# Adding a convolution's taps by accumulating transfers on GpSimd's queue instead of on VectorE

## The chip, the core and the metric

The kernel runs as one launch on one core of a Trainium2 chip (trn2). The metric is the device time of the launch in microseconds (us). The engines are named as in the profile: PE is TensorE (its weight loads are PEld), DVE is VectorE, ACT is ScalarE, POOL is GpSimd, and SP is SyncE, which here only issues transfers. Each engine works through its own instructions in the order in which they were written; across engines and transfers only semaphores order the work.

## What is computed

A decoder trunk of two layers over 256 tokens of width 2048: a gated-linear-attention layer, then a forgetting-attention layer, both with a cross attention into 256 memory tokens, and a channel mixer at the end of each layer. The change touches the channel mixers alone, which are in essence:

```
def causal_dwconv(u, w, b):          # u: (1, 256, 11264)
    up = pad(u, two zero rows ahead)
    return w[0] * up[:, 0:s] + w[1] * up[:, 1:s+1] + w[2] * up[:, 2:s+2] + b

def conv_ffn(h, w_up, conv_w, conv_b, w_down):
    u = causal_dwconv(h @ w_up, conv_w, conv_b)
    a, val = split(u, 2)             # 5632 columns each
    return (silu(a) * val) @ w_down
```

Every column of `h @ w_up` is thus filtered along the tokens with three taps of its own and a bias. All matrix products keep close to full fp32 accuracy: an operand is split into a rounded high part and a low part, and a product is hi*hi + lo*hi + hi*lo on PE.

## The kernel before

**Weights.** The weights stream from HBM in units of 128x1024 words (512 KB). For each unit (`split_unit`, L210 to L235) SP issues the load into one of four `raw` buffers, ACT makes the high part (`whi<-raw`, L233), DVE subtracts it to get the low part (`wlo<-raw,whi`, L234), and PE multiplies with both; `whi` and `wlo` have four buffers each. A cast can thus start when its load has landed and PE has finished with the `whi` of four units ago, and a load can be issued when DVE has finished with the `raw` of four units ago. The casts are issued with a high priority, and the other work of ACT and DVE is tied behind one of them by `tc.issue_after(casts[-1].ins)` or `tc.issue_after(lows[-1].ins)`, so the order of ACT and DVE is, step by step, a cast and then the small work of that step.

**The channel mixer** (`ffn`, L1394). An up step (`up_pair`, L1493) multiplies the 256 tokens with 16 units of `w_up`, in matmuls of 512 columns (L412); one or two pairs of units in it are done with seven block products in place of eight (line L382 casts their weights, L437 to L440 form their sums on DVE). It yields two *turns*, each with two gate and two value chunks of 128 columns. The columns have to lie on the partitions before the convolution and the next product, so each turn is transposed: DVE transposes 32x32 blocks (L1464), POOL's queue sends the tile to HBM and brings it back rearranged (`far_away`, one 512 KB transfer `far<-yu` at L650 and four of 128 KB at L655, `fvt<-far` in the first layer, `yzu<-far` in the second).

**The taps.** When a turn is back, ACT scales it with each tap's weight into three tiles, `tap0` to `tap2` (twelve instructions of 128x256 at L1414: two chunks, gate and value, three taps); `tap1` and `tap2` hold the data shifted by one and two tokens, with zeros ahead. DVE adds `tap1` and then `tap2` to `tap0` in place (`add_tap`, L1421, 128x1024 each). ACT applies silu to the gate half (L1427), DVE multiplies it with the value half (`cv<-tap`, L1434), and the product is split in high and low part (L528 on ACT, L529 on DVE), which become operands of the down product. One set of tap tiles serves all turns.

**What sets the order.** `tick` (L1479) runs once a unit of weights: it gives a credit (1.45, or 1.7 and 2.4 in places) and takes steps from the front of one queue, `waiting`, while credit is left. A tap costs 0.5, an addition 1.0, silu 0.5, the gating 1.0 and 0.7. A turn may be fetched back three ticks after it was sent, and its steps start 8 (or 7) ticks after that, if the steps of the turns before have been taken. There are 44 chunks of columns, so 22 turns in each layer.

## Time and profile before

| | |
|---|---|
| median of 3 runs | 2211.19 us (2211.04 to 2212.21) |
| span of the profiled execution, first to last instruction | 2210.2 us, 1.0 us less than the median |
| PE busy | 2199.2 us |
| DVE busy | 1793.1 us |
| ACT busy | 1421.8 us |
| POOL busy | 136.5 us |
| moved by transfers | 515.41 MB |
| granted TensorE clock | 0.999 of full speed |

The profiled execution is one execution of the program, and the runs are timed apart from it. In the rows of the profile, `L412` is a line of the kernel, `out<-in` are its tiles without their buffer numbers, and `x264` is a count. In a row of a group of instructions, the busy time in us and the mean duration of one in ns follow the first bar, and the idle time of the engine just before them, with what ended it, follows the second. In a timeline a row begins with its start and its duration in us, and a bracket holds the idle time before it and what ended it. A matmul's end is modelled in the profile, so PE's real pace is read from the number of matmuls in a stretch.

### The profile page before, as it was taken

The page shows a single profiled execution, that of the slowest core. Times are in us where ns is not written, and L with a number is a line of the kernel's source. Part 1 is how long each engine was busy: PE and PEld are TensorE (multiplying, and loading weights), DVE is VectorE, ACT ScalarE, POOL GpSimd, SP SyncE. Part 2 cuts the span into 40 slices and gives each one's busy share as a digit, 9 for nine tenths or more (in the row PEclk, how much of TensorE's full clock was granted, in tenths as well). Part 3 has the DMA queues.
Part 4 walks back from the last instruction along what each step waited for, and adds up shares of the span by engine and source line. Part 5 has one row for each costly group of instructions (what it writes and reads, how often), then busy time and mean ns, then how long its engine had stood idle before and what let it go on. Part 6 is the DMA issues. An engine that isn't in the chain of part 4 may idle for free.

```text
span 2210.2 us, 30065 instructions
## 1 busy us (share of the span) xinstructions
PE 2199.2 (100%) x10315; PEld 1851.8 (84%) x10315; DVE 1793.1 (81%) x2655; ACT 1421.8 (64%) x2260; POOL 136.5 (6%) x257
## 2 busy tenths in 40 slices
PE   9999999999999999999999999999999999999998
PEld 7888888888888888888888998888888888888886
DVE  7768977688897889888978669668888888988896
ACT  6655664566787567656865555555788656765874
POOL 0000000001100000001110000000100000100100
PEclk9999999999999999999999999999999999999999
DMA  9867567777677567667678767677777657776774
GB/s 343 259 224 224 190 194 236 252 232 253 227 243 265 187 219 233 231 234 247 222 244 265 231 201 243 225 239 241 228 241 248 234 187 237 243 247 224 227 259 153
DMA packets 166289, 515.41 MB, mean 233 GB/s; under 512 B 20780, under 2 KB 42552, under 8 KB 166136
## 3 DMA queue, kind: packets, MB, share of 16 engines
q1 hardware_dynamic: 149064, 460.99, 63.1%
q0 software_dynamic: 16496, 51.71, 7.5%
q8 instruction: 81, 1.33, 0.2%
q10 hardware_dynamic: 576, 0.79, 0.1%
q14 instruction: 72, 0.59, 0.1%
HBM read 469.62 MB, written 43.79 MB: 232 GB/s over the span
## 4 chain that ended last, share of the span: by engine, by line
PE 99%; DVE 1%; ACT 0%; issue 0%; DVEq 0%; ACTq 0%
PE acc L412 29%; PE acc L338 26%; PE ps_s L412 15%; PE ps_o L412 8%; PE ps_t L412 7%; PE acc L309 3%; PE acc L264 3%; PE ps_s L338 2%; PE acc L368 2%; PE acc L262 1%; PE ps_s L1035 0%; PE ps_o L701 0%; PE ps_s L701 0%; PE ps_s L1308 0%; PE ps_s L1081 0%; PE ps_o L1263 0%
## 5 line engine op out<-in xcount | busy, mean ns | idle before, releaser
L234 DVE TENSOR_TENSOR wlo<-raw,whi 128x1024 fp32r<-128x1024 f32 (+2 forms) x705 | 841.2, 1203 | 241.3 <-ACT whi L233 220.7
L233 ACT ACTIVATE whi<-raw 128x1024 fp32r<-128x1024 f32 (+2 forms) x705 | 729.8, 1046 | 405.4 <-PE acc L338 131.9
L338 PE MATMUL acc<-whi,B 128*128 128x512 f32 (+3 forms) x1248 | 291.7, 370 | 0.0
L382 ACT ACTIVATE whi<-raw 128x1024 fp32r<-128x1024 f32 (+1 forms) x144 | 137.0, 954 | 197.4 <-PE acc L412 75.4
L338 PEld LDWEIGHTS acc<-whi,B 128*128 128x128 f32 x1248 | 226.8, 188 | 28.1
L412 PE MATMUL acc<-whi,mix 128*128 128x512 f32 x756 | 192.9, 389 | 0.0
L412 PE MATMUL acc<-whi,B 128*128 128x512 f32 x738 | 189.8, 389 | 0.0
L383 DVE TENSOR_TENSOR wlo<-raw,whi 128x1024 fp32r<-128x1024 f32 (+1 forms) x144 | 156.2, 1089 | 40.3 <-ACT whi L382 37.2
L412 PEld LDWEIGHTS acc<-whi,mix 128*128 128x128 f32 x756 | 141.9, 188 | 29.5
L412 PEld LDWEIGHTS acc<-whi,B 128*128 128x128 f32 x738 | 138.5, 188 | 28.7
L338 PE MATMUL acc<-wlo,B 128*128 128x512 f32 (+3 forms) x624 | 158.5, 369 | 0.0
L338 PEld LDWEIGHTS acc<-wlo,B 128*128 128x128 f32 x624 | 114.5, 188 | 14.6
L1414 ACT ACTIVATE tap<-fvt,cw 128x256 f32<-128x256 f32 x264 | 123.5, 531 | 2.6 <-DMA fvt<-far 2.5
L1414 ACT ACTIVATE tap<-yzu,cw 128x256 f32<-128x256 f32 x264 | 123.5, 531 | 2.0 <-DMA yzu<-far 2.0
L1421 DVE TENSOR_TENSOR tap<-tap,tap 128x1024 f32<-128x1024 f32 x88 | 107.2, 1219 | 1.4 <-ACT tap L1414 1.0
L412 PE MATMUL ps_s<-whi,mix 128*128 128x512 f32 x386 | 106.2, 389 | 0.0
L412 PE MATMUL acc<-wlo,mix 128*128 128x512 f32 x378 | 105.6, 389 | 0.0
L412 PE MATMUL acc<-wlo,B 128*128 128x512 f32 x369 | 105.1, 389 | 0.0
L412 PE MATMUL ps_s<-whi,B 128*128 128x512 f32 x342 | 93.1, 389 | 0.0
L412 PEld LDWEIGHTS ps_s<-whi,mix 128*128 128x128 f32 x386 | 72.5, 188 | 15.0
L412 PEld LDWEIGHTS acc<-wlo,mix 128*128 128x128 f32 x378 | 70.9, 188 | 14.7
L412 PEld LDWEIGHTS acc<-wlo,B 128*128 128x128 f32 x369 | 69.3, 188 | 14.4
(502 smaller groups left out, 3866.5 us busy)
## 6 DMA issues: line engine op xcount, KB each, us to landing
raw<-wp SPq DMA_DIRECT2D x741, 512.0 KB, 4.6
fvt<-far POOLq DMA_DIRECT2D x100, 128.0 KB, 5.5
raw<-wp SPq DMA_DIRECT2D x32, 384.0 KB, 3.5
far<-yu POOLq DMA_DIRECT2D x22, 512.0 KB, 5.3
far<-yzu POOLq DMA_DIRECT2D x22, 512.0 KB, 5.3
yzu<-far POOLq DMA_DIRECT2D x88, 128.0 KB, 5.5
raw<-wp SPq DMA_DIRECT2D x24, 388.0 KB, 4.4
x<-xtok SPq DMA_DIRECT2D x8, 512.0 KB, 7.2
```

Of the source, the lines that this page charges most:

```text
L233: casts.append(S.activation(hi[:, s], raw[:, s], AF.Copy))
L234: lows.append(V.tensor_tensor(lo[:, s], raw[:, s], hi[:, s].bitcast(F32), ALU.subtract))
L262: mm = TE.matmul(acc[p][c][:, :T], w[:, s], both[:, 0, :], start=False, stop=end and j == 3)
L264: mm = TE.matmul(acc[p][c], w[:, s], both, start=u == j == 0, stop=end and j == 3)
L309: mm = TE.matmul(acc[b][:, :n], src[kcs[j] - base][:, part, b * P : (b + 1) * P], w, start=u == 0 and low == part == j == 0, stop=u == end ...
L338: mm = TE.matmul(acc[b][:, :n], src[kc - base][:, part, b * P : (b + 1) * P], ready[low][:, j * room : j * room + n], start=i == low == pa ...
L368: mm = TE.matmul(acc[b][:, :n], src[kc - base][:, part, b * P : (b + 1) * P], w, start=i == low == part == j == 0, stop=i == end and low = ...
L382: casts.append(S.activation(hi[:, :n], src, AF.Copy))
L383: lows.append(V.tensor_tensor(lo[:, :n], src, hi[:, :n].bitcast(F32), ALU.subtract))
L412: r = TE.matmul(bank[name], x, w, start=name not in begun, stop=last)
L1414: S.activation(by_run(taps[i][:, s, c, i:]), zs[slot][:, :, 2 * c + s], AF.Copy if i else AF.Identity, bias=0.0 if i else w[3], scale=w[2 ...
L1421: V.tensor_tensor(taps[0], taps[0], taps[n][:, :, :, :T], ALU.add)
```

## The change

The two additions of a turn no longer run on DVE. They are two transfers from SBUF to SBUF on POOL's queue which add what they carry to the destination (`accum_op=ALU.add`): first `tap1` onto the sum, then `tap2` onto the sum. Each carries a whole tile, 128x1032 words, 528 KB: all tap tiles get the width 258 for each of their four rows of 256 tokens so that source and destination are flat and of one size, and POOL zeroes the parts that no tap writes. The last two turns of each layer (`j` of 40 and 42) still add on DVE.

The sum has two tiles now, `taps[0]` and `taps[3]`, that serve the turns by turns (`summed(slot)`); `tap1` and `tap2` still have one tile each. The twelve taps are written in another order: `tap0` and `tap1` first, then `tap1` is added, then `tap2` is written and added. Silu and gating go into a second queue of steps, `rear_steps`, and become due four ticks (`ADDED`) after the second addition was issued; `tick` takes a due step of that queue before one of `waiting`. An addition by transfer costs no credit. Finally the program is built with 4096 bytes of SBUF in each partition for the descriptors of POOL's transfers, where it had no such setting before.

On ACT the change moves the taps and silu. This is the piece of the first layer where two turns follow each other; in the kernel before, L233 is the cast, L1414 a tap, L1427 silu, L528 the split of a product:

```order
L528 ACTIVATE A_95<-cv 128x256
L528 ACTIVATE A_96<-cv 128x256
L1414 ACTIVATE tap_4593<-fvt,cw 128x4x2x32 x3
L233 ACTIVATE whi<-raw 128x1024
L1414 ACTIVATE tap_4593<-fvt,cw 128x4x2x32
L233 ACTIVATE whi<-raw 128x1024 x3
L1414 ACTIVATE tap_4594<-fvt,cw 128x4x2x32
L233 ACTIVATE whi<-raw 128x1024
L1414 ACTIVATE tap_4594<-fvt,cw 128x4x2x32 x2
L1427 ACTIVATE tap_4593<-tap_4593 128x2x256
```

Here `tap_4593` is `tap0` and the sum of every turn, and `tap_4594` is `tap1`: the first turn's `tap0` comes last, three casts stand between it and the next turn's first `tap1`, and silu follows. After the change, behind the first turn's last `tap1`, stands this on ACT (L235 is the cast, L1421 a tap, L530 the split; `tap_4594` is `tap1`, `tap_4595` is `tap2`, `tap_4593` the second turn's sum):

```order
L530 ACTIVATE A_95<-cv 128x256
L530 ACTIVATE A_96<-cv 128x256
L235 ACTIVATE whi<-raw 128x1024
L1421 ACTIVATE tap_4595<-fvt,cw 128x4x2x32 x3
L235 ACTIVATE whi<-raw 128x1024
L1421 ACTIVATE tap_4595<-fvt,cw 128x4x2x32
L235 ACTIVATE whi<-raw 128x1024 x2
L1421 ACTIVATE tap_4593<-fvt,cw 128x4x2x32 x4
L235 ACTIVATE whi<-raw 128x1024
L1421 ACTIVATE tap_4594<-fvt,cw 128x4x2x32 x4
L235 ACTIVATE whi<-raw 128x1024 x2
L1421 ACTIVATE tap_4595<-fvt,cw 128x4x2x32 x2
```

The second turn's `tap1` now overwrites what the first turn's first transfer reads, with five casts between, and its `tap2` overwrites what the first turn's second transfer reads.

On POOL, before, the turns alone went out and back:

```order
L650 DMA far<-yu 128x1024
L655 DMA fvt<-far 32x4x256 x4
L650 DMA far<-yu 128x1024
L655 DMA fvt<-far 32x4x256 x4
L650 DMA far<-yu 128x1024
```

After the change, two turns out and back are followed by their four additions, each in the same queue (`tap_4596` is the first turn's sum):

```order
L652 DMA far<-yu 128x1024 x2
L657 DMA fvt<-far 32x4x256 x8
L1429 DMA tap_4596<-tap_4594 128x1032
L1429 DMA tap_4596<-tap_4595 128x1032
L1429 DMA tap_4593<-tap_4594 128x1032
L1429 DMA tap_4593<-tap_4595 128x1032
L652 DMA far<-yu 128x1024
L657 DMA fvt<-far 32x4x256 x4
```

The queue gains 80 transfers in all, and DVE loses 80 of its 88 additions. PE's matmuls, ACT's instructions and SP's transfers keep their numbers.

The whole diff:

```diff
--- before.py
+++ after.py
@@ -36,6 +36,8 @@
 SEVEN_DOWN = {4: 0, 10: 1, 20: 0, 34: 1}
 SEVEN_MORE = 11
 MORE_IN = (5, 6, 8)
+ADDED = 4
+SCRATCH = 4096
 
 
 LEVELS = (64, 16, 4)
@@ -1400,38 +1402,50 @@
             rooms = {i: held("dsum", i) for i in range(2)}
             cw = fp.tile([P, 4 * 88], F32, name="cw")
             nc.sync.dma_start(cw, cnv[l])
-            taps = [fp.tile([P, 2, 2, T + i], F32, name=f"tap{i}") for i in range(3)]
-            for i in (1, 2):
-                nc.gpsimd.memset(taps[i][:, :, :, :i], 0.0)
+            taps = [fp.tile([P, 2, 2, T + 2], F32, name=f"tap{i}") for i in range(4)]
+            for i in range(4):
+                nc.gpsimd.memset(taps[i] if i in (0, 3) else taps[i][:, :, :, : T + 2 : T + 1] if i == 1 else
+                                 taps[i][:, :, :, :i], 0.0)
             count = [0, 0, 0]
             sums = {}
 
+            def summed(slot):
+                return taps[3 * slot]
+
             def tap_of(j, s, c, i, slot):
 
+                t = taps[i] if i else summed(slot)
                 col = (c * 44 + j + s) * 4
                 w = [cw[:, col + n : col + n + 1] for n in range(4)]
                 with tc.issue_after(casts[-1].ins):
-                    S.activation(by_run(taps[i][:, s, c, i:]), zs[slot][:, :, 2 * c + s], AF.Copy if i else AF.Identity,
+                    S.activation(by_run(t[:, s, c, i : T + i]), zs[slot][:, :, 2 * c + s], AF.Copy if i else AF.Identity,
                                  bias=0.0 if i else w[3], scale=w[2 - i])
                 unread[slot] -= 1
 
-            def add_tap(n):
-
+            def add_tap(n, slot, far):
+
+                t = summed(slot)
+                if far:
+                    sent.append(nc.gpsimd.dma_start(flat_tap(t), flat_tap(taps[n]), accum_op=ALU.add))
+                    return
                 with tc.issue_after(lows[-1].ins):
-                    V.tensor_tensor(taps[0], taps[0], taps[n][:, :, :, :T], ALU.add)
-
-            def silu():
-
-                t = taps[0][:, :, 0, :]
+                    V.tensor_tensor(t[:, :, :, :T], t[:, :, :, :T], taps[n][:, :, :, :T], ALU.add)
+
+            def flat_tap(t):
+                return t.rearrange("p s c t -> p (s c t)")
+
+            def silu(slot):
+
+                t = summed(slot)[:, :, 0, :T]
                 with tc.issue_after(casts[-1].ins):
                     S.activation(t, t, AF.Silu)
 
-            def gated(j, s):
+            def gated(j, s, slot):
 
                 if s == 0:
                     product[0] = fp.tile([P, 2, T], F32, name="cv", tag="cv")
                     with tc.issue_after(lows[-1].ins):
-                        V.tensor_tensor(product[0], taps[0][:, :, 0, :], taps[0][:, :, 1, :], ALU.mult)
+                        V.tensor_tensor(product[0], summed(slot)[:, :, 0, :T], summed(slot)[:, :, 1, :T], ALU.mult)
                 r = product[0]
                 with tc.issue_after(lows[-1].ins):
                     split(m, (j + s) % RING, r[:, s, :])
@@ -1465,15 +1479,25 @@
                     if b:
                         away = far_away(dram, flat(y), T, nc.gpsimd)
                         back = lambda: away(flat(z))
-                        steps = [(0.5, lambda s=s, c=c, i=i: tap_of(j, s, c, i, slot)) for n in ((1, 2), (0,))
-                                 for s in range(2) for c in range(2) for i in n]
-                        steps += [(1.0, lambda: add_tap(1)), (1.0, lambda: add_tap(2)), (0.5, silu),
-                                  (1.0, lambda: gated(j, 0)), (0.7, lambda: gated(j, 1))]
+                        far = j < HID // P - 4
+
+                        def taps_of(*n):
+                            return [(0.5, lambda s=s, c=c, i=i: tap_of(j, s, c, i, slot))
+                                    for s in range(2) for c in range(2) for i in n]
+
+                        def ended():
+                            add_tap(2, slot, far)
+                            rear_steps.extend((clock[0] + (ADDED if far else 0), *step) for step in (
+                                (0.5, lambda: silu(slot)), (1.0, lambda: gated(j, 0, slot)),
+                                (0.7, lambda: gated(j, 1, slot))))
+
+                        cost = 0.0 if far else 1.0
+                        steps = [*taps_of(0, 1), (cost, lambda: add_tap(1, slot, far)), *taps_of(2), (cost, ended)]
                         returns.append((clock[0] + 3, slot, back, [(clock[0] + wait, *step) for step in steps]))
 
                 return evac
 
-            waiting, clock, credit = [], [0], [0.0]
+            waiting, rear_steps, clock, credit = [], [], [0], [0.0]
             returns, unread, turned_last = [], [0, 0], [None]
 
             def tick(share):
@@ -1485,8 +1509,11 @@
                     back()
                     unread[slot] = 12
                     waiting.extend(steps)
-                while waiting and waiting[0][0] <= clock[0] and credit[0] > 0:
-                    _, cost, step = waiting.pop(0)
+                while credit[0] > 0:
+                    ready = [q for q in (rear_steps, waiting) if q and q[0][0] <= clock[0]]
+                    if not ready:
+                        break
+                    _, cost, step = ready[0].pop(0)
                     credit[0] -= cost
                     step()
 
@@ -1573,7 +1600,7 @@
                 tick(2.4)
             for _ in wide:
                 tick(2.4)
-            assert not waiting and not returns
+            assert not waiting and not returns and not rear_steps
             if l:
                 for u in range(3, 8):
                     f2(u)
@@ -1787,7 +1814,7 @@
         "par": par,
         "msk": _constants(),
     }
-    nc = bacc.Bacc("TRN2", target_bir_lowering=False, num_devices=1)
+    nc = bacc.Bacc("TRN2", target_bir_lowering=False, num_devices=1, dynamic_dma_scratch_size=SCRATCH)
     aps = [nc.dram_tensor(n, v.shape, mybir.dt.from_np(v.dtype), kind="ExternalInput").ap()
            for n, v in arrays.items()]
     aps.append(nc.dram_tensor("out", (2, P, D), F32, kind="ExternalOutput").ap())
```

## The prediction

> **What bounds the kernel now.** I read the page's busy times first, then PE's waits, then stretches of the two channel mixers, then ACT's timeline in a stretch full of taps.
>
> ```profile
> span 2210.2 us, 30065 instructions
> PE 2199.2 (100%) x10315; PEld 1851.8 (84%) x10315; DVE 1793.1 (81%) x2655; ACT 1421.8 (64%) x2260; POOL 136.5 (6%) x257
> PE ps_o L183 <- DVE B L180: 1.5, 1, 1.5
> PE acc L412 <- ACT whi L382: 0.7, 1, 0.7
> 1922.58 32.64 PE acc L412 x144
> 517.70:1118.60 600.90, 600.19 (x2648) 496.42 (x2647) 515.44 (x607) 423.09 (x642) 56.17 (x103) 1.00 0.70 232
> 1559.00:2140.00 581.00, 581.00 (x2565) 481.07 (x2564) 499.40 (x590) 408.09 (x614) 54.73 (x100) 1.00 0.71 235
> ```
>
> The second row gives each engine's busy time: PE is never free, DVE is free for a fifth. Rows three and four are all of PE's waits: 1.5 us at the start and 0.7 us once in a channel mixer. As a matmul's end is modelled, I check by counting. The chain's row has 144 matmuls in 32.64 us, 0.2267 us each. The last two rows are the stretches from the first to the last tap of the two mixers (length; then busy time and count of PE, PEld, DVE, ACT, POOL; clock; busy share of the transfer engines; GB/s). The first holds 2648 matmuls, and 2648 x 0.2267 = 600.2 of its 600.9 us; the second holds 2565, or 581.4 of 581.0. So PE runs at its own pace, at full clock, and DVE's additions are on no path that sets the end. All that this change can win is that 0.7 us.
>
> What it can lose depends on how far the casts run ahead of PE. ACT's timeline, at a point where two turns' taps are written:
>
> ```profile
> 595.52 1.06 ACT L382 ACTIVATE whi<-raw 128x1024 fp32r<-128x1024 f32 x1 [2.09 <-PE ps_t L412]
> ...
> 600.11 1.06 ACT L382 ACTIVATE whi<-raw 128x1024 fp32r<-128x1024 f32 x1 [2.49 <-DVE raw L438]
> ...
> 602.04 1.06 ACT L382 ACTIVATE whi<-raw 128x1024 fp32r<-128x1024 f32 x1 [0.25 <-DVE raw L440]
> 603.01 1.05 ACT L233 ACTIVATE whi<-raw 128x1024 fp32r<-128x1024 f32 x1
> ...
> 605.00 1.30 ACT L1414 ACTIVATE tap<-fvt,cw 128x256 f32<-128x256 f32 x3
> 606.20 1.05 ACT L233 ACTIVATE whi<-raw 128x1024 fp32r<-128x1024 f32 x1
> 607.15 1.30 ACT L1414 ACTIVATE tap<-fvt,cw 128x256 f32<-128x256 f32 x3
> ...
> 625.16 0.71 ACT L528 ACTIVATE mix<-cv 128x256 fp32r<-128x256 f32 x2
> 625.78 0.59 ACT L1414 ACTIVATE tap<-fvt,cw 128x256 f32<-128x256 f32 x1
> ...
> 630.20 1.07 ACT L233 ACTIVATE whi<-raw 128x1024 fp32r<-128x1024 f32 x1 [0.46 <-PE acc L412]
> 590.23 1.22 DVE L1421 TENSOR_TENSOR tap<-tap,tap 128x1024 f32<-128x1024 f32 x1
> 595.03 1.22 DVE L1421 TENSOR_TENSOR tap<-tap,tap 128x1024 f32<-128x1024 f32 x1
> ```
>
> At 595.52 and 630.20 the cast waited for PE to free a buffer, so there it was as far ahead as four buffers allow. In between it was not. The cast at 595.52 opens when PE has left the `whi` of four units ago; ahead of it stand two whole units and a half-wide one of the seven-product pair (12, 12 and 3 matmuls) and the 4 low matmuls of the unit being left: 31 x 0.2267 = 7.0 us, so PE needs it at 602.5. The two casts after it serve 6 matmuls each, as it does, so the cast of 603.01 is needed 18 x 0.2267 = 4.1 us later, at 606.6, and that of 606.20 one unit (2.7 us) later, at 609.3. They end at 604.1 and 607.3: a lead of 2.0 to 2.5 us. It is short because the cast at 600.11 waited 2.49 us for DVE's weight sums, and ahead of these DVE had just done two of the additions that now go (2.4 us, the last two rows).
>
> **The change part by part.**
>
> *What goes from DVE.* The far turns are those with `j` below 40: 20 a layer, 40 in all, two additions each.
>
> ```profile
> L1421 DVE TENSOR_TENSOR tap<-tap,tap 128x1024 f32<-128x1024 f32 x88 | 107.2, 1219 | 1.4 <-ACT tap L1414 1.0
> far<-yu POOLq DMA_DIRECT2D x22, 512.0 KB, 5.3
> far<-x SPq DMA_DIRECT2D x8, 512.0 KB, 3.4
> fvt<-far POOLq DMA_DIRECT2D x100, 128.0 KB, 5.5
> q0 software_dynamic: 16496, 51.71, 7.5%
> 594.03 2.18 POOL L655 DMA_DIRECT2D fvt<-far  x4 [5.28 <-DMA far<-yu]
> 632.42 0.56 POOL L650 DMA_DIRECT2D far<-yu  x1 [25.28 <-DVE yu L1464]
> ```
>
> 80 x 1.219 = 97.5 us leave DVE. All of it was beside PE's work, so it is worth nothing by itself; it only lengthens the lead where DVE was late, by up to the 2.4 us above. I take a lead of 3 us in such a stretch.
>
> *What comes: 80 accumulating transfers of 528 KB.* No row shows one. From below I bound its landing by the quickest 512 KB rows, SP's store at 3.4 us. From above: q0 is POOL's queue, and 7.5% of 16 engines' span of 2210.2 us for 51.71 MB makes 2652 engine-us, 27.1 for 0.528 MB, or 1.7 us of all 16 engines. If adding costs as much as three more passes, it lands after 5.3 + 3 x 1.7 = 10.4 us. I take one more pass, since the destination has to be read too: 5.3 + 1.7 = 7.0 us, with the row of the same queue and nearly the same size as its base.
>
> The Trainium skill ("Collectives: The Full Stack", section "The bandwidth ceiling: the fold count and why AG ≠ RS ≠ AR") says that an addition inside a transfer costs no cycles but needs two source reads, which halves the rate; no run here shows it. Its page "DMA: Bandwidth & Descriptors" (section on the anatomy of one SWDGE transfer) fits 2.0 us + bytes/436e3, an estimate of 3.2 us for 528 KB, or 4.4 with a second read; then ACT would not wait at all. The trace has 5.3 us for the plain transfer of 512 KB beside the weight stream, so the page's floor is too low here.
>
> *Where ACT waits for them.* On ACT, after the first turn's last `tap1`, stand (order above) a pair of splits, five casts, four `tap2` and four first taps of the second turn before its first `tap1`. By the timeline's starts a cast takes 0.95 us, a tap 0.40 and the pair 0.62: 0.62 + 5 x 0.95 + 8 x 0.40 = 8.6 us. The first transfer has landed by then (7.0). Up to the second turn's first `tap2` come four taps and two casts more, 3.5 us, so 12.1 us. The second transfer writes the same sum as the first and can be issued only when that has landed, so it lands after 2 x 7.0 = 14.0 us. ACT waits 1.9 us there, with taps and all later casts queued behind it, and then DVE's low parts and PE behind those. A lead of 3 us covers that, and nothing reaches PE; without it, 20 pairs of far turns at 1.9 us would cost 38 us. The second turn's silu needs all four transfers, 4 x 7.0 = 28 us from the start of the count; it stands seven casts or more behind that `tap2`, 7 x 2.72 = 19 us at PE's pace, so at 31 us: covered.
>
> *POOL's queue.* Behind the four additions stands the next `far<-yu`, which waited 25.28 us for DVE's transposes before. The additions take that room. The first can go at about 610 (eight taps after 605.00, in three steps), the fourth when three have landed, at 631, and `far<-yu` right behind it: just in time for 632.42. Behind that, four `fvt<-far` issued in 2.18 us from 594.03 land at about 601 by the median of 5.5 us, and the first tap that reads them ran at 605.00, so some 3 us of delay would be hidden (its slack, by these rows).
>
> *The transfer engines.* 80 x 27.1 x 2 = 4336 engine-us, 271 us of 16 engines, spread over some 1075 us of the two stretches (20 of 22 turns): the share goes from 0.70 to 0.95. That is high, yet the loads' lateness falls into stretches where they had landed early, since ACT is behind in them.
>
> *The smaller descriptor space and the zeroing.* I cost both at nothing: POOL issues four transfers within 2.18 us with no wait, its new zeroing stands in a queue that is idle for tens of us, and both bounds of the descriptor space are below as a rival.
>
> *Sum.* 2210.2 + 0 - 0.7 at most; with the 1.0 us between the span and the median, 2211 us.
>
> **The rivals.** *The additions land late (slower).* PE is hit from the point where twice the landing exceeds 12.1 + 3 us: from 7.6 us. At 8 us it is 0.9 us for each of 20 pairs, +18 us, 2229; at 9 us 2.9 each, +58, 2269; at the upper bound 5.7 each, +114, 2325. For it speaks that `fvt<-far` takes 5.5 us for a quarter of the bytes; against it that the destination is SBUF and not HBM. *The transfer engines fill (slower).* With three passes more the share passes 1.0 by a fifth: 0.70 + 4 x 0.126 = 1.20, and weights come at PE's pace no longer, 0.20 x 1075 = +215 us, 2426. *POOL runs out of descriptor space (slower).* If each of the four 128 KB transfers had to drain before the next, a turn would come back after 4 x 5.5 = 22 us in place of 7.7; less the 3 us hidden and the lead of 3 that leaves 8 us for each of 22 pairs, +180, about 2390. Nothing in the profile shows such a wait, and none shows how near it is. *Faster by more than 0.2%.* It would need matmuls to run faster than 0.2267 us, and the counts above show every stretch at that pace. *The change does not do what it says.* The order has the 80 transfers and 80 additions fewer on DVE, so this is out.
>
> **How the numbers follow.** 0.2% is 4.4 us, about what a measurement of this kernel can tell from no change. No change: 0.58, all from the forecast. Late additions 0.29, full transfer engines 0.06, descriptor space 0.05: slower 0.40. Faster 0.02, as only 0.7 us is there to win. The forecast is 2211, its own range 2209 to 2215. Half of the late cases and a little more lie below 9 us of landing, so up to 2270 the range holds 0.58 + 0.02 + about 0.2 of the 0.29.
>
> **What would show it.** Right: PE's waits still about 2 us, 2648 matmuls in 601 us, DVE's busy time near 1696 us, ACT waiting at `tap` for the additions by 0 to 3 us a pair, a landing of 6 to 7.5 us. Wrong: casts that start late because a `tap` ahead of them waited for the transfer into its tile, and PE waiting for `whi`; or casts waiting for `raw<-wp`, with a transfer share near 1; or POOL's `fvt<-far` spaced wider than 0.55 us.

## The result, and the profile after

The changed kernel takes 2264.19 us (median of four runs, 2263.28 to 2269.19) against 2211.7 us for the kernel before in the same session: a ratio of 1.024, with a 95% interval of 1.0228 to 1.0253. It is 52 us slower, where no change was forecast. One execution of experiment 15 below ran at a granted clock of 0.917, took 2290.84 us and is left out of that experiment's time.

The page of the changed kernel (the profiled execution spans 2262.5 us, 52.3 more than before):

```profile
span 2262.5 us, 30174 instructions
PE 2219.0 (98%) x10315; PEld 1851.8 (82%) x10315; DVE 1708.1 (75%) x2575; ACT 1420.9 (63%) x2260; POOL 212.0 (9%) x341
q0 software_dynamic: 28016, 93.98, 17.4%
tap<-tap POOLq DMA_DIRECT2D x80, 516.0 KB, 7.6
```

(The page's KB have 1024 bytes: 516.0 KB is the whole tap tile of 528 KB.) Its waits of PE and of ACT (us in all, how often, the longest):

```profile
PE acc L414 <- ACT whi L384: 9.5, 8, 2.6
PE ps_o L414 <- ACT whi L235: 9.2, 7, 3.1
...
ACT whi L235 <- DMA raw<-wp: 91.8, 77, 6.5
...
ACT tap L1421 <- DMA tap<-tap: 50.0, 21, 5.0
...
ACT tap L1441 <- DMA tap<-tap: 34.4, 6, 7.2
```

The line on landing in the view of the `tap` tiles, over the whole execution:

```profile
DMA to landing us min/median/max: 4.5/7.6/12.7
```

And the stretch of the first mixer that the prediction counted (columns as there):

```profile
517.70:1118.60 600.90, 585.61 (x2548) 477.14 (x2546) 451.23 (x544) 400.64 (x603) 91.15 (x141) 1.00 0.85 259
```

In the same 600.90 us PE now does 2548 matmuls, where it did 2648: 100 x 0.2267 = 22.7 us behind in this stretch alone. So PE has real gaps now. Each is small (the longest 3.1 us), and most of them end with a cast. On ACT two new rows stand beside the ones known from before: 50.0 us of waits at the taps and 34.4 us at silu (L1441), both for the landing of an addition. ACT's own work has not grown (1420.9 us).

One place shows the whole chain, in the timeline of the changed kernel at a pair of turns in the second mixer:

```profile
1728.06 0.94 POOL L1429 DMA_DIRECT2D tap<-tap  x1 [6.73 <-ACT B L530]
...
1736.40 0.88 POOL L1429 DMA_DIRECT2D tap<-tap  x1 [7.41 <-DVE wlo L236]
...
1740.47 0.50 ACT L1421 ACTIVATE tap<-yzu,cw 128x256 f32<-128x256 f32 x1
...
1745.19 0.91 ACT L1421 ACTIVATE tap<-yzu,cw 128x256 f32<-128x256 f32 x2 [4.22 <-DMA tap<-tap]
1746.00 1.04 ACT L235 ACTIVATE whi<-raw 128x1024 fp32r<-128x1024 f32 x1
...
1747.10 0.74 PE L414 MATMUL ps_o<-whi,mix 128*128 128x512 f32 x2 [3.08 <-ACT whi L235]
```

The first turn's additions are issued at 1728.06 and, when the first has landed, at 1736.40. (The brackets on POOL name other engines, but those had long been done; of the 8.3 us between the two, 7.8 are the landing of the first.) At 1740.97 ACT is through with the second turn's `tap1` and wants to write `tap2`, which the second transfer still reads. It lands 8.7 us after its issue, ACT goes on at 1745.19, 4.22 us late, and the cast behind the taps starts at 1746.00. PE stood still for 3.08 us until it had that `whi`.

The stop costs more than its length. Two stretches behind it, in the columns of the stretch above:

```profile
1748.60:1752.00 3.40, 3.40 (x9) 2.64 (x8) 3.40 (x6) 3.22 (x6) 1.40 (x2) 0.50 0.57 172
1752.00:1755.40 3.40, 3.40 (x16) 2.82 (x15) 3.40 (x5) 1.06 (x1) 0.00 (x0) 1.00 1.03 225
```

For 3.4 us PE was granted half the clock and did 9 matmuls in place of 16. The changed kernel has four such stretches ahead of its last few us, each beginning within 2 us behind a stop of 1.4 to 3.2 us (other stops of that length have none), and the kernel before has none. At half the clock they cost 4 x 1.7 = 6.8 us. The granted clock of the whole execution, 0.996 against 0.999, says the same.

The starts of PE's matmuls give an account of all its stops. Counted is by how much a matmul starts later than 0.2267 us behind the one before it, from 0.25 us on; a stop is put down to an addition when ACT waited for one in the 10 us before it. In the changed kernel the stops come to 39.7 us (2.0 us before): 17.8 behind a tap that waited for an addition, 10.7 behind a silu that did, 11.1 behind neither. Of the 11.1, 4.4 stand behind a tap that waited for its turn and some 2.5 behind a cast that waited for its weights. This sorts by nearness in time; the experiments have to show the cause.

### The profile page after: what moved, and what is told of

It is laid out like the page before. It is cut to its first block, busy times and chain, and to the rows that moved or that the text cites. A ratio compares the mean times of both kernels' runs of the same rounds, so it can differ in the third digit from the quotient of the medians.

```text
span 2262.5 us, 30174 instructions
## 1 busy us (share of the span) xinstructions
PE 2219.0 (98%) x10315; PEld 1851.8 (82%) x10315; DVE 1708.1 (75%) x2575; ACT 1420.9 (63%) x2260; POOL 212.0 (9%) x341
## 3 DMA queue, kind: packets, MB, share of 16 engines
q0 software_dynamic: 28016, 93.98, 17.4%
## 5 line engine op out<-in xcount | busy, mean ns | idle before, releaser
L235 ACT ACTIVATE whi<-raw 128x1024 fp32r<-128x1024 f32 (+2 forms) x705 | 731.6, 1045 | 387.1 <-PE acc L340 128.8
L1421 ACT ACTIVATE tap<-fvt,cw 128x256 f32<-128x256 f32 x264 | 123.4, 533 | 33.7 <-DMA tap<-tap 26.5
L1421 ACT ACTIVATE tap<-yzu,cw 128x256 f32<-128x256 f32 x264 | 123.1, 532 | 32.5 <-DMA tap<-tap 23.4
L340 PEld LDWEIGHTS acc<-wlo,B 128*128 128x128 f32 x624 | 114.5, 188 | 14.7
L1429 POOL DMA_DIRECT2D tap<-tap x80 | 70.6, 883 | 463.9 <-ACT tap L1421 218.0
L414 PE MATMUL ps_o<-whi,mix 128*128 128x512 f32 x222 | 71.9, 398 | 10.9 <-ACT whi L235 7.4
## 6 DMA issues: line engine op xcount, KB each, us to landing
tap<-tap POOLq DMA_DIRECT2D x80, 516.0 KB, 7.6
```

Of the source, the lines that this page charges most:

```text
L235: casts.append(S.activation(hi[:, s], raw[:, s], AF.Copy))
L340: mm = TE.matmul(acc[b][:, :n], src[kc - base][:, part, b * P : (b + 1) * P], ready[low][:, j * room : j * room + n], start=i == low == pa ...
L414: r = TE.matmul(bank[name], x, w, start=name not in begun, stop=last)
L1421: S.activation(by_run(t[:, s, c, i : T + i]), zs[slot][:, :, 2 * c + s], AF.Copy if i else AF.Identity, bias=0.0 if i else w[3], scale=w[2 ...
L1429: sent.append(nc.gpsimd.dma_start(flat_tap(t), flat_tap(taps[n]), accum_op=ALU.add))
```

## The experiments

Each is compared with the kernel before, measured on the same chip in the same session. The theory after this reading: ACT waits for two additions that land one behind the other, and casts are queued behind it. The rivals: the load that the additions put on the transfer engines makes the weights late; the small descriptor space; and the order of the steps, which the change also alters. Experiments 2 and 3 keep the order of the change on every engine; in the others a cast and a small instruction change places here and there, so differences of a few us are not read.

**1. All additions back on DVE**; the order of the taps, the two sums and the second queue of steps stay.

```diff
-                if far:
-                    sent.append(nc.gpsimd.dma_start(flat_tap(t), flat_tap(taps[n]), accum_op=ALU.add))
-                    return
```

> The changed kernel with all additions back on DVE; the order of the taps, the two sums, the second queue of steps and the 4096 bytes of descriptor space stay. Theory of waits (ACT, in order, stands before a tap or a silu until an addition has landed, and the casts behind it come late): back to 2211 to 2214 us. Theory of load (the added transfers take the transfer engines from the weights): the same, 2211 to 2214. Theory of the descriptor space (POOL's transfers start later with 4096 bytes): still above 2225. Theory of the order (the taps written in one run and the later gating load ACT too densely): near 2264.

2221.16 us, a ratio of 1.0038 (1.0024 to 1.0052), which lies in none of the expected ranges. The row of its page on POOL's queue, and that of its waits on the casts that wait for weights:

```profile
q0 software_dynamic: 16496, 51.71, 7.6%
```

```profile
ACT whi L235 <- DMA raw<-wp: 96.2, 66, 4.8
```

The same waits in the kernel before, and there the taps' wait for a turn that comes back:

```profile
ACT whi L233 <- DMA raw<-wp: 56.0, 48, 3.4
...
ACT tap L1414 <- DMA fvt<-far: 2.5, 2, 2.4
```

So some 8 us of the 52 (8.4 by the ratio, 9.8 by the medians) have nothing to do with transfers. And the waits of casts for weights, which stood at 56.0 us before and at 91.8 after, stand at 96.2 here, without any added transfer: the order of the steps alone brings a rise of that size, so it is no sign of load.

**2. Plain copies in place of additions.** The same 80 transfers in the same order, without the adding, so the convolution's sums are not formed.

```diff
-                    sent.append(nc.gpsimd.dma_start(flat_tap(t), flat_tap(taps[n]), accum_op=ALU.add))
+                    sent.append(nc.gpsimd.dma_start(flat_tap(t), flat_tap(taps[n])))
```

> The changed kernel with plain copies in place of the accumulating transfers, in the same order on every engine; the sums are wrong, since each copy overwrites instead of adding. Waits: the landing falls from 7.6 to about 5.5 us, two in a row take 11 us against the 12.1 us that ACT gives, so most of the loss goes: 2212 to 2226 us. Load: the added engine time is halved, and so is the loss: 2230 to 2245. Descriptor space: no change, 2258 to 2268.

2220.66 us, 1.0038 (1.0024 to 1.0051), the time of experiment 1. From its page and its waits:

```profile
q0 software_dynamic: 28016, 93.98, 12.5%
tap<-tap POOLq DMA_DIRECT2D x80, 516.0 KB, 5.9
```

```profile
ACT tap L1421 <- DMA tap<-tap: 6.4, 6, 2.4
ACT tap L1441 <- DMA tap<-tap: 4.0, 2, 3.4
```

That the transfers add, rather than copy, thus costs 43 us. A copy lands in 5.9 us and not 7.6, and ACT's waits for it are 10.4 us and not 84.4. From the issue of a pair's first copy to the landing of the second it is 12.0 us in the median (worked out from the issue and landing of each), and 15.7 us for the additions; the prediction had counted 12.1 us of room on ACT. The price of adding itself follows from the shares of q0: 17.4% of 16 engines x 2262.5 us less 7.6% of 16 x 2221.1 is 3598 engine-us for 80 additions, 45.0 each; 12.5% of 16 x 2214.1 less the same is 1727 for 80 copies, 21.6 each. The Trainium skill ("Collectives: The Full Stack", section "The bandwidth ceiling: the fold count and why AG ≠ RS ≠ AR") says of the reduce step of a collective that its addition needs two source reads and so runs at half the rate of a copy. In engine time the traces agree: 45.0 / 21.6 = 2.08. Whether two reads are the reason, no run here shows.

**3. Twice the descriptor space.**

```diff
-SCRATCH = 4096
+SCRATCH = 8192
```

> The changed kernel with 8192 bytes of descriptor space instead of 4096, nothing else, in the same order on every engine. Descriptor space: at least half of the loss goes, 2238 us or less, and the first packet of an addition starts 1 to 2 us after its issue and no longer 3 to 5. Waits and load: 2260 to 2268, as before.

2265.37 us, 1.0238 (1.0216 to 1.026): no different from the change. Experiments 1 and 8 have 4096 bytes too and lose little or nothing. That rival is out.

**4. The load without the waits, first attempt.** Additions on DVE, and 80 accumulating transfers onto a spare tile that nobody reads, each behind a small POOL copy that waits for the taps.

```diff
...
-                    sent.append(nc.gpsimd.dma_start(flat_tap(t), flat_tap(taps[n]), accum_op=ALU.add))
-                    return
+                    mark = sm.tile([P, 1], F32, name="mark", tag="mark", bufs=6)
+                    with tc.issue_after(casts[-1].ins):
+                        S.activation(mark, taps[n][:, 1, 1, T - 1 : T], AF.Copy)
+                    nc.gpsimd.tensor_copy(taps[4][:, 0, 0, :1], mark)
+                    sent.append(nc.gpsimd.dma_start(flat_tap(taps[4]), flat_tap(taps[4]), accum_op=ALU.add))
```

> All additions on DVE as in the first run, and beside them 80 accumulating transfers of the same size onto a spare tile that nobody reads, each behind a small POOL copy that waits for the taps; ACT gets 80 tiny instructions more (some 0.2 us each). Waits: no instruction of ACT or DVE waits for them, so 2211 to 2218 us. Load: the weights come late as in the changed kernel, above 2240; POOL's queue is held up by them as in the changed kernel, so what late turns cost shows here too.

2352.92 us, 1.0641 (1.0625 to 1.0657), far above either expectation. Its waits say why it answers another question:

```profile
ACT tap L1422 <- DMA fvt<-far: 70.4, 8, 11.8
ACT tap L1422 <- DMA yzu<-far: 61.3, 8, 11.2
...
PE acc L414 <- ACT whi L235: 53.2, 8, 7.2
```

All 80 now wrote one tile, each waiting for the one before, and the turns that have to go out and come back stood behind them in POOL's queue. ACT waited for the *turns*, 131.7 us, where the kernel before has 2.5 us in the row shown above. So the load stays unmeasured here, but a second way to lose is shown: whatever waits in POOL's queue makes the next turn late.

**5. A `tap1` and a `tap2` of its own for each sum**, so that nothing is overwritten under a running transfer (and 512 bytes less descriptor space to make room).

```diff
...
-                t = taps[i] if i else summed(slot)
+                t = taps[3 * slot + i]
...
```

> The changed kernel with tap1 and tap2 in two tiles each, one for each of the two sums (descriptor space 3584 bytes to make room), so that no tap overwrites what a transfer still reads; silu still waits for both additions four ticks after the second. The load on the transfer engines stays. Waits: the waits of ACT before taps (50.0 us in the changed kernel) go, those before silu (34.4 us) stay or grow, so between a third and three quarters of the loss goes: 2228 to 2250 us. Load: no change, 2258 to 2270.

2263.59 us, 1.0227 (1.0212 to 1.0242): nothing gained, and by its time alone a point for the load. The wait at the taps is gone from its waits, and the one at silu has nearly doubled from 34.4:

```profile
ACT tap L1441 <- DMA tap<-tap: 61.2, 18, 6.5
ACT tap L1421 <- DMA fvt<-far: 17.3, 4, 7.2
```

The overwriting was only the first place at which ACT met a late addition.

**6 and 7. Silu eight ticks after the second addition in place of four**, with own tiles (6) and with one tile each (7). With eight ticks the down product multiplies some pieces of the gated product before they are written.

```diff
-ADDED = 4
+ADDED = 8
```

> The same with silu and gating eight ticks after the second addition instead of four, so that ACT has no reason left to wait for an addition, while all 80 accumulating transfers stay. Waits: about what the order alone costs, 2214 to 2226 us. Load: the accumulating packets still take twice a copy's time on the transfer engines, so 2250 us or more.

> The changed kernel with eight ticks in place of four before silu, one tile each for tap1 and tap2 as it was. Waits: the 34.4 us before silu go, the 50.0 us before taps stay: 2240 to 2258 us. Load: no change, 2258 to 2270.

2270.9 us (1.0248 to 1.0282) and 2274.77 us (1.0258 to 1.0313). In 6 the waits for additions are down to 16.2 us; in their place stand these:

```profile
ACT tap L1421 <- DMA yzu<-far: 23.6, 5, 7.3
ACT tap L1421 <- DMA fvt<-far: 19.0, 5, 7.4
PE acc L414 <- ACT mix L530: 5.8, 2, 4.3
PE ps_o L414 <- ACT more L530: 4.7, 1, 4.7
```

A later silu makes the product late for PE (`mix` and `more` are its pieces), and the turns are late as in experiment 4. The times are no point for the waits: 6 is where the load was to have it, 7 above both expectations. By the rows the loss moved from one wait to the next and did not shrink.

**8. Only the second addition by a transfer**, the first on DVE: 40 transfers, one a turn.

```diff
-                if far:
+                if far and n == 2:
```

> The changed kernel with the first addition of a turn on DVE and only the second as a transfer: 40 accumulating transfers, none of which has to wait for another on the same sum. Waits: one landing of 7 to 8 us against about 9 us on ACT before the next tap2, so little beside the order's cost: 2214 to 2228 us. Load: half of what the accumulation costs over the order, 2238 to 2246 us.

2214.24 us over ten runs, 1.0008 (0.9999 to 1.0017): nothing that can be told from no change. Half of the transfers cost far less than half of the loss, and one landing takes as long as in the change:

```profile
tap<-tap POOLq DMA_DIRECT2D x40, 516.0 KB, 7.5
```

```profile
ACT tap L1421 <- DMA tap<-tap: 7.0, 9, 1.6
```

**9. Load that nobody waits for.** Experiment 1 with 160 plain 512 KB stores of an idle tile, four behind each far turn on POOL's queue.

```diff
...
-                        back = lambda: away(flat(z))
...
+                        def back():
+                            away(flat(z))
+                            for _ in range(4 if far else 0):
+                                spot = dram.tile([P, 4 * T], F32, name="spot", tag="spot", bufs=16)
+                                with tc.issue_after(sent[-1].ins):
+                                    sent.append(nc.gpsimd.dma_start(spot, idle))
...
```

> All additions are on DVE as in the first experiment, which took 2221; POOL's queue also stores a tile that nobody needs to spare places in HBM, four times 512 KB behind each of the 40 far turns. 160 such stores at about 160 ns a packet load the transfer engines about as much as the 80 accumulating transfers at 331 ns a packet do, and no instruction waits for them. If the loss comes from the waits for two additions one behind the other, the time is near that of the first experiment, 2217 to 2226. If it comes from the load on the transfer engines, the weights come late, ACT's waits at the casts for raw<-wp grow well past 96 us, and the time is 2240 or more.

2244.88 us, 1.0152 (1.0138 to 1.0166): 33 us over the kernel before, some 24 over experiment 1. This is a miss for the theory of waits alone, and by its own words a point for the load:

```profile
q0 software_dynamic: 39536, 135.60, 16.9%
```

```profile
ACT whi L235 <- DMA raw<-wp: 141.9, 102, 4.3
PE ps_o L414 <- DVE wlo L236: 6.3, 7, 1.8
```

Much the same share of the engines as the change's 17.4% does cost time here. But it comes in bunches of four, and it shows where load should show: casts wait 141.9 us for weights, 46 more than in experiment 1. The change has 91.8. The load of this size can hurt; in the change its mark is not seen.

**10. Long waits with little load.** Each addition replaced by two plain copies of a quarter of the tile, one behind the other (the sums are not formed).

```diff
-                    sent.append(nc.gpsimd.dma_start(flat_tap(t), flat_tap(taps[n]), accum_op=ALU.add))
+                    for _ in range(2):
+                        sent.append(nc.gpsimd.dma_start(t[:, 0, 0, :], taps[n][:, 0, 0, :]))
```

> Each addition is replaced by two plain copies of a quarter of the tile, one behind the other, since both write the same place (the sums are thus wrong): together less than half the packet time of one accumulating transfer, but two landings in a row where there was one. If the wait decides, two landings of 4 to 5 us each are 8 to 10 us for one addition, longer than the 7.6 us of the change: 2250 or more. If the load decides, the time is below that of the plain copies, 2215 to 2225.

2232.82 us, 1.0094 (1.0066 to 1.0122), between the two expectations, so neither holds by itself:

```profile
tap<-tap POOLq DMA_DIRECT2D x160, 129.0 KB, 4.1
```

```profile
ACT tap L1442 <- DMA tap<-tap: 29.5, 6, 6.7
ACT tap L1421 <- DMA tap<-tap: 28.4, 14, 4.4
```

Two landings of 4.1 us are 8.2 in place of 7.6, yet ACT waits 57.9 us and not 84.4. With fewer bytes than the copies of experiment 2 it is 12 us slower than these, so waits without load do cost time; they cost less than the change.

**11. Two additions in a chain, but only for the first turn of a pair**, the second adds on DVE: 40 transfers, as in experiment 8.

```diff
-                        far = j < HID // P - 4
+                        far = j < HID // P - 4 and slot == 1
```

> Of the two turns of a pair only the first has its two additions by transfers, the second adds on DVE: 40 transfers, as many as in the eighth experiment, which lost nothing at 2214, but two in a chain. If the chain of two landings in front of the next turn's taps decides, the waits at taps for tap<-tap stay at about half or more of the 50 us of the change, and the time is 2225 to 2250. If only the number of transfers decides, it is 2212 to 2220.

2261.9 us, 1.0228 (1.0214 to 1.0242): the whole loss, with half of the transfers.

```profile
q0 software_dynamic: 22256, 72.84, 12.5%
tap<-tap POOLq DMA_DIRECT2D x40, 516.0 KB, 6.6
```

```profile
ACT tap L1421 <- DMA tap<-tap: 44.3, 21, 6.1
```

Against experiment 8 the bytes are the same, the landing is even shorter (6.6 against 7.5 us), and 48 us lie between them. What differs is that the two transfers of a turn go one behind the other, in front of the next turn's taps.

**12. The order with its credit given back**: experiment 1 with a credit of 1.0 for an addition and silu due at once.

```diff
-ADDED = 4
+ADDED = 0
...
-                        cost = 0.0 if far else 1.0
+                        cost = 1.0
```

> The first experiment (all additions on DVE) with the credit of 1.0 for an addition given back and silu due at once; the order of taps and the two sums stay. The first experiment was 9 us over the kernel before. If these 9 us come from additions that cost no credit and from the delay of four ticks, the time is 2210 to 2215; if they come from the order of the taps and the two sums, it stays at 2217 to 2223.

2214.99 us over eleven runs, 1.0016 (1.0007 to 1.0025). Of the 8 us that the order cost, some 5 come from additions that cost no credit and from the four ticks; 3 us stay with the order of the taps and the two sums.

**13. The chain where no taps follow it**: as 11, but the *second* turn of each pair by transfers.

```diff
-                        far = j < HID // P - 4
+                        far = j < HID // P - 4 and slot == 0
```

> As the eleventh experiment (2262), but the second turn of each pair has its additions by transfers and the first adds on DVE: the same 40 transfers in chains of two, with no next turn's taps close behind them. If the loss is ACT waiting to overwrite tap1 and tap2, ACT's waits at taps for tap<-tap fall from 44 us to under 10 and the time is 2212 to 2225. If the chain's load or its place in POOL's queue costs the time, it stays at 2245 to 2270.

2230.8 us, 1.0078 (1.0058 to 1.0098), 31 us less than experiment 11, with the same number of transfers in the same chains of two, which land more slowly:

```profile
tap<-tap POOLq DMA_DIRECT2D x40, 516.0 KB, 8.4
```

```profile
ACT tap L1441 <- DMA tap<-tap: 16.9, 8, 5.9
```

No row for the taps is left among ACT's waits for additions, as expected; the time misses the expected 2225 by 6 us. So the place of the chain carries most of experiment 11's 50 us.

**14. Experiment 11 with own tiles**, as in experiment 5.

> As the eleventh experiment, with a tap1 and a tap2 of its own for each of the two sums, so that nothing is overwritten under a running transfer. If the overwriting alone costs the time, 2212 to 2225. If silu, which needs both landings, takes the wait over as it did in the fifth experiment, ACT waits for tap<-tap at silu by 30 us or more and the time is 2240 to 2265.

2237.09 us, 1.0111 (1.0096 to 1.0126). The overwriting is worth 25 of the 50 us. Silu took over part of the wait, 22.5 us in 12 times, less than the 30 expected, and the time is below that expectation too.

**15. More distance on ACT**: the change with a credit of 1.0 for each transferred addition.

```diff
-                        cost = 0.0 if far else 1.0
+                        cost = 1.0
```

> The change with a credit of 1.0 for each transferred addition in place of 0: load and chains are those of the change, but the taps of a pair are spread over more units, about 0.7 of a unit of 2.7 us for each addition, so the second turn's first tap2 comes some 3 to 4 us later after the first turn's tap1. If the waits decide, ACT's 84 us of waits for tap<-tap fall to less than half and the time is 2215 to 2240; if the load decides, it stays at 2255 or more.

2235.05 us (the median of three executions), 1.0105 (1.0089 to 1.0122). All 80 transfers and all chains stay, and half of the loss is gone.

**16 and 17. Own tiles (the edit of 5) and the credit together** (16), and silu at six ticks as well (17).

```diff
-                        cost = 0.0 if far else 1.0
+                        cost = 1.0
...
-ADDED = 4
+ADDED = 6
```

> The change with a tap1 and a tap2 of its own for each sum and the credit of 1.0 for each transferred addition: all 80 transfers stay, nothing is overwritten under them, and silu has more distance. If the waits decide, ACT waits for tap<-tap by under 20 us in all and the time is 2214 to 2232, below the fifteenth experiment's 2237. If the load decides, it is as there, 2235 or more, although the waits are gone.

> As the sixteenth experiment, with silu due six ticks behind the second addition in place of four. If the waits decide, ACT's waits for tap<-tap are near 0 and the time is 2212 to 2228, unless the product comes too late for PE, which shows as PE waiting for mix or more. If the load decides, it is 2235 or more with PE waiting for casts that wait for raw<-wp.

16 takes 2235.55 us, 1.0107 (1.009 to 1.0124), no better than 15, though ACT waits 19.8 us for additions in place of 84.4: by its expectation a point for the load. Its trace says where the remainder is lost:

```profile
ACT tap L1421 <- DMA yzu<-far: 11.6, 5, 5.4
ACT tap L1421 <- DMA fvt<-far: 11.1, 5, 4.3
```

Counted as above, PE's stops come to 16.4 us. None stands behind a wait for an addition; 11.4 us stand within 10 us behind a tap that waited for its turn, and 3.5 us are waits for late pieces of the product. A turn's way out (`far<-yu`) lands after 8.5 us, where it took 5.3 us before and 5.4 in experiment 1. So the 80 transfers cost time here through the turns, which share POOL's queue with them, and hardly through the weights. Whether that is the order of the queue or the load, no run separates. 17 takes 2269.32 us, 1.0259 (1.0244 to 1.0274), which neither theory had. No wait for an addition is left in it; POOL and ACT of 17:

```profile
596.66 0.85 POOL L1429 DMA_DIRECT2D tap<-tap  x1 [8.49 <-issue]
597.20 1.40 POOL L652 DMA_DIRECT2D far<-yu  x2
607.90 4.38 POOL L657 DMA_DIRECT2D fvt<-far  x8 [9.30 <-DMA far<-yu]
614.02 1.49 ACT L1421 ACTIVATE tap<-fvt,cw 128x256 f32<-128x256 f32 x3 [6.79 <-DMA fvt<-far]
```

Here both turns of the next pair stand behind all four additions, go out together at 597.20, and come back so late that ACT waits 6.79 us for the first of them. In 8 of the 20 groups of four additions in 16 one of the two goes out ahead of the fourth addition, in 17 in 2. The order on POOL alone does not decide it: in the change all 20 groups stand ahead of both turns, and ACT waits 16.2 us for turns in place of 62.8. But it is experiment 4's kind of loss: with the direct waits gone, POOL's queue is the next that is late.

## Why the prediction was wrong

*PE is saturated, and DVE's additions are on no path.* Right. There was nothing to win, and DVE's 85.0 us of less busy time bought nothing. (97.5 us were forecast from the sum of the durations; the profile counts overlapping instructions once, and DVE's durations before sum to 1958 us in 1793.1 us of busy time.)

*The landing of an addition, 7.0 us.* This is the first of the terms that failed. It measured 7.6 us, within the bounds of 3.4 to 10.4. The reasoning behind it held: adding takes twice the engine time of a copy. The estimate of 4.4 us, worked out there from the Trainium skill ("DMA: Bandwidth & Descriptors", section "Anatomy of one DMA — SWDGE (gpsimd) path"), lies further off than the rows of the trace did. 7.6 is exactly the landing from which the prediction's own rival had PE hit, and the step took a spread of 4.5 to 12.7 us for one number. A chain of two took 15.7 us in the median against the 14.0 forecast (11.9 to 20.5).

*12.1 us of room on ACT.* Right: from the issue of a pair's first addition to the point where ACT is ready for the second turn's first `tap2` it is 12.0 us in the median of the 20 pairs (11.1 to 17.5), and copies whose chains take 12.0 us cost 10.4 us of waits, against 84.4.

*A lead of 3 us covers the wait.* This is the second term that failed, and the more serious one. Of 4.22 us at ACT, 3.08 reached PE in the place shown. Over the pairs, PE stopped behind 11 of ACT's waits for a chain, and what was covered of each was 0.6 to 2.8 us, 1.8 in the median; one wait of 3.13 us was covered whole. The lead before was read as 2.0 to 2.5 us, and it was raised because DVE's additions go, which by the prediction's reading had made its weight sums late. The casts' wait for these sums did not fall with them (before, then after):

```profile
ACT whi L382 <- DVE raw L438: 30.0, 13, 3.8
...
ACT whi L384 <- DVE raw L440: 39.9, 14, 4.7
```

So no run shows the raise. Experiment 15, worth 29 us, does not test this term: its credit widens the room, from 12.0 us to 17.8 in the trace of experiment 16, which has the same credit.

The two terms together are worth some 18 us, what PE lost behind waiting taps. They do not make up the 52 us: the other 10.7 us behind silu, the 8 us of the order and the 6.8 us of the halved clock (shares that may overlap) stand in no term of the sum, or in one put at nothing.

*The order itself and the clock.* No terms of the sum. The order is 8 us (experiment 1), most of it the credit and the delay (experiment 12). That a stop of PE is followed by matmuls at half the clock could not be seen in a trace where PE's longest wait in the mixers was 0.7 us.

*Silu is covered, 28 against 31 us.* Wrong: 34.4 us of waits in the change and 61.2 us as soon as the taps no longer waited (experiment 5). In the pair shown it was covered, in six other places not.

*POOL's queue comes just in time, 3 us of slack.* Nearly right: the taps' waits for their turns rose from 4.5 to 16.2 us, and 4.4 us of PE's stops stand behind them. It was right in that there was nothing to spare: experiments 4, 6, 16 and 17 lost time there.

*The engines' share rises from 0.70 to 0.95, hidden.* It rose to 0.85 in the first stretch; an addition costs 45.0 engine-us and not 54. That it is hidden is neither shown nor refuted in full. Experiments 8, 11 and 13 set it aside as the main cause: at the same number of bytes they are at 2214, 2262 and 2231 us. But experiment 9 shows that a like load in bunches can cost 24 us, there through late weights. In the change only some 2.5 us of PE's stops stand behind a cast that waited for weights. The load can also act by making the landings of the additions and the turns longer, and how much of the change's 52 us is load in that way stays open; no run here takes the waits away and leaves the load as evenly spread as the change has it, without also moving POOL's queue.

*The descriptor space and the zeroing.* At nothing, as forecast (experiment 3 for the space; experiment 8 has both and is at 2214 us).

The rival that came true is the one called late additions, at 0.29; its signs, casts behind a waiting tap and PE waiting for `whi`, are those of the profile. The chance for no change was too high because two terms near a threshold were each taken at one value, with the favourable rounding for the lead. That 2264 us lies below the 2270 up to which it gave 0.8 is luck: at the landing of 7.6 us its formula for late additions gives 20 x (15.2 - 15.1) = 2 us.

## What to carry to other kernels

Work that leaves a free engine for a queue of transfers trades a cost that nobody waited for against a latency that somebody does: count, for each tile it holds, how long until the next writer wants it, and compare that with the whole chain of landings at its slow end, not with the median of one. One landing a turn was free here, and two in a row ahead of the next turn's taps cost the whole loss, 31 us more than the same two behind them. Where instructions stand in order behind the waiting one, taking away the first wait only shows the next, at silu, at the product, or at the next turn behind the same queue.

## What the runs showed of the hardware

An accumulating transfer between SBUF tiles took twice the engine time of a copy (45.0 against 21.6 engine-us for 516 KB), but its landing rose only from 5.9 to 7.6 us. The landing of like transfers moved by a factor of nearly three in one execution (4.5 to 12.7 us), which a median hides. Behind some of its stops of 1.4 us and more PE was granted half the clock for 3.4 us, so that a stop of 3.08 us cost 1.7 us on top.
